# Splitting the input weights of layer 1's mixer ahead of time and reading the parts back from DRAM, in a two-layer diffusion trunk

## The chip, the core and the metric

The kernel runs on one core of a Trainium2 chip. The metric is device time in microseconds (us) of one execution; lower is better. The engines are PE (TensorE), DVE (VectorE), ACT (ScalarE), POOL (GpSimd) and SP (SyncE). SP computes nothing here; it issues most of the DMAs. All DMAs of the core run on 16 DMA engines.

## What is computed

The reference is a trunk of two layers over 512 latent tokens and 256 context tokens of width 1024, all in float32. Cut to what matters here:

```python
def odd_mixer(hl, hc, w_in, ...):                  # layer 1; w_in is 1024 x 2048
    gate_l, xr_l = jnp.split(hl @ w_in, 2, axis=-1)
    gate_c, xr_c = jnp.split(hc @ w_in, 2, axis=-1)
    xr_l, xr_c = depthwise_conv(xr_l, ...), depthwise_conv(xr_c, ...)
    for d, reverse in ((0, False), (1, True)):     # gated linear recurrence over time
        a_c, u_c = rglru_inputs(xr_c, ...); h_c = rglru_scan(a_c, u_c, 0, reverse)
        a_l, u_l = rglru_inputs(xr_l, ...); hs_l.append(rglru_scan(a_l, u_l, h0, reverse))
    y_lat = (gelu(gate_l) * (hs_l[0] + hs_l[1])) @ w_out

def trunk_layer(x, xc, ...):
    y_l, y_c = mixer(modulate(x), modulate(xc))
    x = layer_norm(ALPHA * x + g1 * y_l)
    x = layer_norm(ALPHA * x + g2 * (square(relu(modulate(x) @ mlp_w1)) @ mlp_w2))
    ...                                            # layer 0 does the same for the context xc
```

Layer 0's mixer is attention beside an RWKV-7 scan, layer 1's the recurrent block above. Each layer ends with a squared-ReLU feed-forward of width 4096.

## The kernel before

**Products.** Every large product runs as three: each float32 operand is split into a high part, rounded to PE's fp32r format, and a low part, the rest; `mm3` (L174) adds high by high, low by high and high by low. A weight comes in tiles of 1024 x 128, that is 128 partitions x 8 x 128, 512 KB. `w_raw` (L149) loads a tile into a buffer `wraw` by a DMA of SP, whose pieces are rows of 512 bytes. `w_split` (L155) makes the parts by `split` (L125): ACT casts to `whi`, DVE subtracts into `wlo`. There are 2 buffers `wraw` and 3 each of `whi` and `wlo`. `w_tiles` (L163) does this tile after tile and calls `fill` behind each.

**Layer 1's mixer** (`layer1_mixer`, L549) takes the 16 tiles of `l1_w_in` as they are needed: 8 for the x branch (`xt`, function `dense`, 768 tokens) and 8 for the gate (`gt`, function `gate`, 512 tokens). Block b of 128 channels goes from `dense` (PE), copies into `xp` (ACT), a convolution (`cy`, ACT and DVE), a split of its result, four small products (`tr`, PE), tanh, exp and sqrt (`ga`, `gx`, `tv`, ACT, with table loads between them), and multiplications and scans (DVE). The gate tile of the block is multiplied in at the end, `ge`.

**Fillers.** Work that belongs to a later stage is kept in a list, `self.fillers`; `fill` takes one entry each time that a weight tile has been split. In layer 0's feed-forward the entries are 40 steps of `mods_dve` (L260), which work out a part of layer 1's modulation on DVE (`macc`), from `mraw` tiles. `paced` puts each step behind the last product that was recorded:

```python
def paced(self, gen):
    with self.tc.issue_after(self.pace.ins):
        next(gen)
```

It ties an instruction of the step to that product on the engine of the product, PE; what a step puts on ACT, DVE, POOL or SP isn't tied.

**What sets the order.** The program is recorded in the order of the code, and a scheduler with a timeline of its own then orders each engine's instructions by when it holds them ready. Each engine runs its list strictly in order, and an instruction at the head that waits for a semaphore holds all behind it, DMA issues too.

**The stage around 800 to 930 us.** The RWKV scan of layer 0 ends there. `out_proj` (L697) follows in two halves of 384 tokens, 8 weight tiles of `l0_w_out` each. Behind each half stands `ln_half` (L368), the layer norm: per 128 tokens statistics on DVE, `lnrs` (a power, on POOL), `xn` (ACT), transposes (`tr`, PE), then `hf` (ACT), `hhi` and `t` (DVE) and `hlo` (DVE, and POOL for k in 1, 3, 5). Then the feed-forward `mlp` (L399) begins, with `mr` and `uhi` on ACT, `msq` and `ulo` on DVE. At the end of the scan the stage's inputs come back from DRAM (`t<-o_scr`, `t<-tsp`). The pool `mt`, in which the change puts its buffers, opens with this stage.

Of the kernel before, what the change touches and what calls it, by code (L numbers as in the profile page):

```python
# [10 lines left out]
F32 = mybir.dt.float32  # L11
F32R = mybir.dt.float32r
# [5 lines left out]
D = 1024  # L18
# [9 lines left out]
def run(*gens):  # L28

    gens = list(gens)  # L30
    while gens:
        gens = [g for g in gens if next(g, gens) is not gens]


def weave(tc, dense, lead):

    for ins in lead:
        with tc.issue_after(ins.ins):
            next(dense, None)
    run(dense)  # L40
# [13 lines left out]
class Kern:  # L54
# [108 lines left out]
    def w_tiles(self, ap, group=128, eng=("act", "dve")):  # L163

        K, M = ap.shape
        kt = K // 128
        for c0 in range(0, M, group):
            g = min(group, M - c0)
            raw = self.w_raw(ap[:, c0:c0 + g], kt, g)
            for s in range(0, g, 128):  # L170
                yield (c0 + s) // 128, self.w_split(raw[:, :, s:s + 128], *eng)
                self.fill()

    def mm3(self, out, st, mv, ks, first=True, last=True):  # L174

# [334 lines left out]
XW = XO + NC_  # L510

EARLY = {1: 1, 2: 1, 3: 1, 4: 1, 5: 1, 6: 1}
XS, GS, OS = ("act", "dve"), ("act", "dve"), ("act", "dve")
GE, HS, GW = 2, 4, 1
PREG = 2

# [1 line left out]
class L1(Kern):  # L518
# [30 lines left out]
    def layer1_mixer(self, hhi, hlo, ohi, olo, late):  # L549
        nc = self.nc  # L550
        I = self.I
        with self.tc.tile_pool(name="m1", bufs=1, reuse_waits="tile") as m1:
            self.l1_softplus()
            ea, et, ba, bx = self.lru_e
            spans = ((0, NL, 0), (NL, T, XO))
            w_in = I["l1_w_in"]
            cw = self.cols["l1_conv_w"]
            xps = [m1.tile([128, XP], F32, name=f"xp{i}") for i in range(2)]
            for xp in xps:
# [91 lines left out]
                nc.vector.tensor_tensor(out=hs[b], in0=g["gx", 0][:, :NL], in1=g["gx", 1][:, :NL], op=ALU.add)  # L651

            hs, last, prev = {}, {}, [None, None]
            xt, gt = self.w_tiles(w_in[:, D:2 * D], eng=XS), self.w_tiles(w_in[:, 0:D], eng=GS)

            def gates(n):
                for _ in range(n):
# [22 lines left out]
            with self.tc.issue_after(last[7].ins):  # L680
                run(late)
# [859 lines left out]
class Trunk(L1, MLA, RWKV):  # L1541
    def run(self, out):
        nc, tc, I = self.nc, self.tc, self.I
# [21 lines left out]
        with ExitStack() as s0:  # L1565
# [4 lines left out]
            with ExitStack() as s1:  # L1570
# [3 lines left out]
                with ExitStack() as s2:  # L1574
# [3 lines left out]
                    t = tp.tile([128, 8, T], F32, name="t0")  # L1578
# [42 lines left out]
        with ExitStack() as s0:  # L1621
# [3 lines left out]
            with ExitStack() as s1:  # L1625
# [4 lines left out]
                t = tp.tile([128, 8, T], F32, name="t_0")  # L1630
# [15 lines left out]
                spare = chain(*[self.mods_dve(1, b) for b in range(0, MODV, 2)])  # L1646
                self.fillers += [lambda: self.paced(spare)] * (MODV // 2 * 5)
                self.fillers += [lambda b=b: run(self.mods_spare(1, [b])) for b in range(MODV, 16)]
                lnl = []
                t_spill = self.dram.tile([128, 8, NL], F32, name="t_spill")  # L1650

# [19 lines left out]
            t = tp.tile([128, 8, NL], F32, name="t_1")  # L1671
# [26 lines left out]
```

## Time and profile before

| | us |
|---|---|
| median of 3 runs (lowest, highest) | 2102.24 (2087.21, 2103.8) |
| the profiled execution | 2098.16 |
| its span in the trace | 2096.2 |

| engine | busy us | share of the span |
|---|---|---|
| PE | 1933.4 | 92% |
| DVE | 1264.6 | 60% |
| ACT | 828.6 | 40% |
| POOL | 382.4 | 18% |

The span is the stretch of the trace; 1.96 us of the execution lie outside it. Times below count from the span's start. Of the median, the profiled execution is 4.1 us short. PE's clock was granted at 0.962 of full speed on the mean.

### The profile page before, as it was taken

The page shows a single profiled execution, that of the slowest core. Times are in us where ns is not written, and L with a number is a line of the kernel's source. Part 1 is how long each engine was busy: PE and PEld are TensorE (multiplying, and loading weights), DVE is VectorE, ACT ScalarE, POOL GpSimd, SP SyncE. Part 2 cuts the span into 40 slices and gives each one's busy share as a digit, 9 for nine tenths or more (in the row PEclk, how much of TensorE's full clock was granted, in tenths as well). Part 3 has the DMA queues.
Part 4 walks back from the last instruction along what each step waited for, and adds up shares of the span by engine and source line. Part 5 has one row for each costly group of instructions (what it writes and reads, how often), then busy time and mean ns, then how long its engine had stood idle before and what let it go on. Part 6 is the DMA issues. An engine that isn't in the chain of part 4 may idle for free.

```text
span 2096.2 us, 39749 instructions
## 1 busy us (share of the span) xinstructions
PE 1933.4 (92%) x16130; PEld 1729.7 (83%) x16130; DVE 1264.6 (60%) x2532; ACT 828.6 (40%) x1437; POOL 382.4 (18%) x441
## 2 busy tenths in 40 slices
PE   7889788799999997999999999999989889999997
PEld 4667566577777767899999999998877789999997
DVE  4548777647676678775554333447698575444446
ACT  2344242434554443442131221334789444233242
POOL 0346644534435431100000000001000010000000
PEclk8999889799999998999999999999989989999999
DMA  9455534554423218332232222245521663333334
GB/s 347 122 167 191 144 106 129 153 137 127 125 57 95 61 53 264 102 91 81 81 102 84 67 61 61 61 131 152 151 76 56 203 190 101 92 96 96 98 100 146
DMA packets 429303, 249.20 MB, mean 119 GB/s; under 512 B 79376, under 2 KB 414144, under 8 KB 428992
## 3 DMA queue, kind: packets, MB, share of 16 engines
q1 hardware_dynamic: 428648, 245.55, 40.0%
q8 instruction: 127, 2.08, 0.4%
q0 software_dynamic: 288, 1.05, 0.2%
q14 instruction: 56, 0.46, 0.1%
q10 hardware_dynamic: 184, 0.06, 0.0%
HBM read 209.38 MB, written 36.44 MB: 117 GB/s over the span
## 4 chain that ended last, share of the span: by engine, by line
PE 69%; DVE 10%; DMA 8%; ACT 5%; issue 3%; POOL 2%; SPq 2%; DVEq 0%; ACTq 0%; POOLq 0%
PE mm L183 17%; PE mm L184 17%; PE mm L185 17%; PE tr L183 2%; DVE wlo L136 2%; PE tr L184 1%; ACT whi L130 1%; DMA wraw<-in_l_w_out_dram 1%; PE tr L185 1%; PE mm L883 1%; PE mm L874 1%; PE g L1389 1%; DMA st<-rw_pq 1%; PE g L1366 1%; DMA wraw<-in_l_mlp_w_dram 1%
## 5 line engine op out<-in xcount | busy, mean ns | idle before, releaser
L183 PE MATMUL mm<-hhi,whi 128*128 128x384 f32 (+2 forms) x1504 | 489.1, 326 | 2.7 <-DVE msq L427 2.0
L184 PE MATMUL mm<-hlo,whi 128*128 128x384 f32 (+2 forms) x1504 | 485.8, 323 | 0.2 <-DVE hlo L396 0.2
L185 PE MATMUL mm<-hhi,wlo 128*128 128x384 f32 (+2 forms) x1504 | 485.5, 323 | 0.0
L130 ACT CAST whi<-wraw 128x1024 fp32r<-128x1024 f32 x216 | 226.2, 1049 | 529.7 <-PE mm L184 449.0
L183 PE MATMUL mm<-uhi,whi 128*128 128x384 f32 (+1 forms) x1280 | 399.4, 313 | 4.4 <-DVE t L450 4.2
L185 PE MATMUL mm<-uhi,wlo 128*128 128x384 f32 (+1 forms) x1280 | 397.8, 311 | 3.6 <-DVE wlo L136 3.6
L184 PE MATMUL mm<-ulo,whi 128*128 128x384 f32 (+1 forms) x1280 | 397.2, 311 | 1.0 <-DVE ulo L136 1.0
L136 DVE TENSOR_TENSOR wlo<-wraw,whi 128x1024 fp32r<-128x1024 f32 x216 | 267.6, 1240 | 204.4 <-ACT whi L130 202.7
L183 PEld LDWEIGHTS mm<-hhi,whi 128*128 128x128 f32 x1504 | 285.7, 190 | 15.7 <-issue 2.3
L184 PEld LDWEIGHTS mm<-hlo,whi 128*128 128x128 f32 x1504 | 285.7, 190 | 11.2 <-issue 1.4
L185 PEld LDWEIGHTS mm<-hhi,wlo 128*128 128x128 f32 x1504 | 285.6, 190 | 10.5 <-issue 0.2
L183 PEld LDWEIGHTS mm<-uhi,whi 128*128 128x128 f32 x1280 | 243.8, 191 | 6.0 <-DVE t L450 4.4
L185 PEld LDWEIGHTS mm<-uhi,wlo 128*128 128x128 f32 x1280 | 243.3, 190 | 5.8 <-DVE wlo L136 4.9
L184 PEld LDWEIGHTS mm<-ulo,whi 128*128 128x128 f32 x1280 | 243.4, 190 | 1.8 <-DVE ulo L136 1.5
L450 DVE SCALAR_TENSOR_TENSOR t<-mm,g,t 128x256 f32<-128x256 f32 (+2 forms) x200 | 92.9, 481 | 224.9 <-PE mm L185 222.0
L347 POOL TENSOR_TENSOR lnrs<-lnrs,mhalf 128x1 f32<-128x1 f32 x20 | 10.7, 544 | 1010.1 <-DVE lnrs L346 1010.1
L1411 POOL TENSOR_SCALAR ds<-rv,rw_dd 64x64 f32<-64x64 f32 x176 | 84.6, 481 | 158.8 <-DVE rv L1425 148.9
L427 DVE SCALAR_TENSOR_TENSOR msq<-mm,mr 128x384 f32<-128x384 f32 (+1 forms) x128 | 62.3, 487 | 46.8 <-ACT mr L425 46.6
L425 ACT ACTIVATE mr<-mm 128x384 f32<-128x384 f32 (+1 forms) x128 | 55.6, 434 | 85.4 <-PE mm L185 85.3
L130 ACT CAST uhi<-msq 128x384 fp32r<-128x384 f32 (+1 forms) x128 | 58.6, 458 | 75.6 <-DVE msq L427 75.6
L136 DVE TENSOR_TENSOR ulo<-msq,uhi 128x384 fp32r<-128x384 f32 (+1 forms) x128 | 63.0, 492 | 33.1 <-ACT uhi L130 29.5
L1425 DVE SCALAR_TENSOR_TENSOR rv<-z,rw_dd,ds 64x64 f32<-64x64 f32 x176 | 49.7, 282 | 28.0 <-PE z L1423 23.2
(416 smaller groups left out, 3016.4 us busy)
## 6 DMA issues: line engine op xcount, KB each, us to landing
wraw<-in_l_mlp_w_dram SPq DMA_DIRECT2D x148, 512.0 KB
mraw<-in_l_mod_w_dram SPq DMA_DIRECT2D x48, 512.0 KB
wraw<-in_l_w_in_dram SPq DMA_DIRECT2D x36, 512.0 KB
wraw<-in_l_w_out_dram SPq DMA_DIRECT2D x32, 512.0 KB
mw<-in_l_mod_w_dram SPq DMA_DIRECT2D x16, 512.0 KB
wraw<-in_l_mod_w_dram SPq DMA_DIRECT2D x16, 512.0 KB
rw_bk<-pqbk SPq DMA_DIRECT2D x8, 768.0 KB
rw_pq<-pqbk SPq DMA_DIRECT2D x8, 768.0 KB
```

What stands on the lines that cost most here:

```text
L130: nc.scalar.copy(hi, src)
L136: e.tensor_tensor(out=lo, in0=src, in1=hi.bitcast(F32), op=ALU.subtract)
L183: nc.tensor.matmul(out, sh, mh, start=f, stop=False)
L184: nc.tensor.matmul(out, sh, ml, start=False, stop=False)
L185: ins = nc.tensor.matmul(out, sl, mh, start=False, stop=l)
L425: nc.scalar.activation(r, ps, AF.Relu)
L427: nc.vector.scalar_tensor_tensor(out=sq, in0=ps, scalar=0.0, in1=r, op0=ALU.max, op1=ALU.mult)
L450: nc.vector.scalar_tensor_tensor(out=t[:, m, x:y], in0=ps[:, x - a:y - a], scalar=g[:, m, s:s + 1], in1=t[:, m, x:y], op0=ALU.mult, op1=AL ...
L874: nc.tensor.transpose(ps[:, j * 128:(j + 1) * 128], p[:, (j0 + j) * 128:(j0 + j + 1) * 128], self.ident)
L883: nc.tensor.matmul(po[64 * e:64 * e + 64, :256], va[:, k0 // 128 + j, h * 64:(h + 1) * 64], pts[e][:, j, :], start=(j == 0), stop=(j == n ...
L1411: P.tensor_scalar(out=ds[d][H[e]], in0=rv[H[e], i, e, :], scalar1=dn[H[e]], scalar2=None, op0=ALU.mult)
L1425: V.scalar_tensor_tensor(out=rn[H[e], e, :], in0=zu[d][H[e], 1], scalar=dn[H[e]], in1=ds[d][H[e]], op0=ALU.mult, op1=ALU.add)
```

## The change

The 16 tiles of layer 1's `w_in` are no longer loaded and split in the mixer. A generator `presplit` does it before: per tile a load into `praw`, the same cast on ACT (`phi`) and subtraction on DVE (`plo`), and two DMAs that write the parts to a DRAM tensor `w_pre`, [16, 2, 128, 8, 128], in which each partition's part is one row of 4 KB. All three DMAs of a tile are issued on POOL's queue (`nc.gpsimd`), not on SP's. `praw`, `phi` and `plo` have one buffer each. Its 17 steps are queued as paced fillers behind the 40 of before. In the mixer `w_pre` loads `whi` and `wlo` directly, by two DMAs of SP of 512 KB each.

```diff
@@ class Kern, behind w_tiles @@
+    def presplit(self, ap, n):
+        nc = self.nc
+        self.pre = self.dram.tile([n, 2, 128, 8, 128], F32, name="w_pre")
+        sb = lambda tag, dt: self.mt.tile([128, 8, 128], dt, tag=tag, name=self.nm(tag), bufs=1)
+
+        def load(j):
+            raw = sb("praw", F32)
+            nc.gpsimd.dma_start(raw, ap[:, 128 * j:128 * j + 128].rearrange("(k p) c -> p k c", p=128))
+            return raw
+
+        raw = load(0)
+        yield
+        for j in range(n):
+            hi, lo = sb("phi", F32R), sb("plo", F32R)
+            self.split(hi, lo, raw)
+            if j + 1 < n:
+                raw = load(j + 1)
+            for i, x in enumerate((hi, lo)):
+                nc.gpsimd.dma_start(self.pre[j, i], x.bitcast(F32))
+            yield
+
+    def w_pre(self, js):
+        for i, j in enumerate(js):
+            w = [self.wp.tile([128, 8, 128], F32R, tag=t, name=self.nm(t), bufs=self.wbufs[1]) for t in ("whi", "wlo")]
+            for u, x in enumerate(w):
+                self.nc.sync.dma_start(x.bitcast(F32), self.pre[j, u])
+            yield i, w
@@ layer1_mixer @@
-            w_in = I["l1_w_in"]
...
-            xt, gt = self.w_tiles(w_in[:, D:2 * D], eng=XS), self.w_tiles(w_in[:, 0:D], eng=GS)
+            xt, gt = self.w_pre(range(8, 16)), self.w_pre(range(8))
@@ Trunk.run, layer 0's feed-forward, behind the two lines that queue mods_dve and mods_spare @@
+                ahead = self.presplit(I["l1_w_in"], 16)
+                self.fillers += [lambda: self.paced(ahead)] * 17
```

**POOL, layer 0's output projection and first layer norm.** `ulo` is the last split before it, `lnrs` and `hlo` belong to the layer norm. Before, POOL's list reads:

```order
L136 TENSOR_TENSOR ulo1381_9058<-t_0_9056,uhi1380_9057 128x768 x2
L347 TENSOR_TENSOR lnrs1420_9365<-lnrs1420_9365,mhalf_62 128x1
L347 TENSOR_TENSOR lnrs1426_9386<-lnrs1426_9386,mhalf_62 128x1
L347 TENSOR_TENSOR lnrs1432_9407<-lnrs1432_9407,mhalf_62 128x1
L396 TENSOR_TENSOR hlo1384_9088<-hf1437_9426,hhi1383_9087 128x384
L396 TENSOR_TENSOR hlo1384_9088<-hf1440_9443,hhi1383_9087 128x384
L396 TENSOR_TENSOR hlo1384_9088<-hf1443_9460,hhi1383_9087 128x384
L347 TENSOR_TENSOR lnrs1484_9770<-lnrs1484_9770,mhalf_62 128x1
```

After, it reads like this from the write of the third tile's high part on (lines of the changed code: L182 is the load, L193 the writes, L377 `lnrs`):

```order
L193 DMA w_pre_12719<-phi1874_12986 128x1024
L182 DMA praw1876_12990<-in_l1_w_in_dram 128x8x128
L193 DMA w_pre_12719<-plo1875_12987 128x1024
L193 DMA w_pre_12719<-phi1882_13053 128x1024
L377 TENSOR_TENSOR lnrs1420_9365<-lnrs1420_9365,mhalf_62 128x1
L377 TENSOR_TENSOR lnrs1426_9386<-lnrs1426_9386,mhalf_62 128x1
L182 DMA praw1884_13057<-in_l1_w_in_dram 128x8x128
L193 DMA w_pre_12719<-plo1883_13054 128x1024
L193 DMA w_pre_12719<-phi1890_13120 128x1024
L182 DMA praw1892_13124<-in_l1_w_in_dram 128x8x128
L193 DMA w_pre_12719<-plo1891_13121 128x1024
L377 TENSOR_TENSOR lnrs1432_9407<-lnrs1432_9407,mhalf_62 128x1
```

The 48 DMAs of `presplit` now stand between the `ulo` of the scan's end and the second layer norm's first `lnrs`: eleven ahead of the first layer norm's first `lnrs`, the last seven behind its last `hlo`, and the others between its `lnrs` and `hlo`.

**ACT, the same stage.** `whi` are the splits of the output projection's weights, `xn` and `hf` the layer norm's. Before, ACT's list reads:

```order
L130 CAST whi1460_9556<-wraw1459_9554 128x1024
L357 ACTIVATE xn1422_9370<-tr1417_9351,lnnm1421_9368,lnrs1420_9365 128x1024
L357 ACTIVATE xn1428_9391<-tr1423_9372,lnnm1427_9389,lnrs1426_9386 128x1024
L130 CAST whi1464_9591<-wraw1463_9589 128x1024
L357 ACTIVATE xn1434_9412<-tr1429_9393,lnnm1433_9410,lnrs1432_9407 128x1024
L130 CAST whi1468_9626<-wraw1467_9624 128x1024
L390 ACTIVATE hf1436_9421<-tr1435_9414,a1_0B_9040,a1_0G_9039 128x384
L390 ACTIVATE hf1437_9426<-tr1435_9414,a1_0B_9040,a1_0G_9039 128x384
L390 ACTIVATE hf1439_9438<-tr1438_9431,a1_0B_9040,a1_0G_9039 128x384
L130 CAST whi1472_9663<-wraw1471_9661 128x1024
```

After, with `phi` as the presplit's cast, it reads:

```order
L130 CAST whi1452_9517<-wraw1451_9515 128x1024
L130 CAST phi1882_13053<-praw1876_12990 128x1024
L130 CAST whi1460_9556<-wraw1459_9554 128x1024
L387 ACTIVATE xn1422_9370<-tr1417_9351,lnnm1421_9368,lnrs1420_9365 128x1024
L387 ACTIVATE xn1428_9391<-tr1423_9372,lnnm1427_9389,lnrs1426_9386 128x1024
L130 CAST whi1464_9591<-wraw1463_9589 128x1024
L130 CAST phi1890_13120<-praw1884_13057 128x1024
L130 CAST whi1468_9626<-wraw1467_9624 128x1024
L387 ACTIVATE xn1434_9412<-tr1429_9393,lnnm1433_9410,lnrs1432_9407 128x1024
L130 CAST phi1898_13187<-praw1892_13124 128x1024
L420 ACTIVATE hf1436_9421<-tr1435_9414,a1_0B_9040,a1_0G_9039 128x384
L420 ACTIVATE hf1437_9426<-tr1435_9414,a1_0B_9040,a1_0G_9039 128x384
```

Of the 16 casts `phi`, the first stands behind the third `whi` of the output projection, these three around the first half's layer norm, and the last among the first `mr` and `uhi` of the feed-forward's first chunk; between `xn` and `hf` a `phi` has come in.

**SP, the end of layer 0's feed-forward.** The last `wraw` loads of `mlp_w2` lead over to layer 1. Before, SP's list reads:

```order
L152 DMA wraw2065_14511<-in_l0_mlp_w2_dram 128x8x128
L152 DMA wraw2161_15000<-in_l1_w_in_dram 128x8x128
L152 DMA wraw2166_15059<-in_l1_w_in_dram 128x8x128
L1658 DMA t_spill_9885<-t_0_9056 1024x1x384
L152 DMA wraw2171_15118<-in_l1_w_in_dram 128x8x128
L152 DMA wraw2176_15151<-in_l1_w_in_dram 128x8x128
L247 DMA mraw2111_14738<-in_l1_mod_w_dram 128x8x128
L152 DMA wraw2197_15257<-in_l1_w_in_dram 128x8x128
L247 DMA mraw2115_14755<-in_l1_mod_w_dram 128x8x128
```

After, with L201 as the read of a part, it reads:

```order
L152 DMA wraw2113_14640<-in_l0_mlp_w2_dram 128x8x128
L152 DMA wraw2465_16736<-in_l1_w_out_dram 128x8x128
L152 DMA wraw2469_16768<-in_l1_w_out_dram 128x8x128
L1689 DMA t_spill_9885<-t_0_9056 1024x1x384
L201 DMA whi2209_15129<-w_pre_12719 128x1024
L201 DMA wlo2210_15130<-w_pre_12719 128x1024
L201 DMA whi2213_15186<-w_pre_12719 128x1024
L201 DMA wlo2214_15187<-w_pre_12719 128x1024
L201 DMA whi2217_15243<-w_pre_12719 128x1024
L201 DMA wlo2218_15244<-w_pre_12719 128x1024
L277 DMA mraw2159_14867<-in_l1_mod_w_dram 128x8x128
```

In place of one load of 512 KB a tile there are two, into `whi` and `wlo`; the free `wraw` buffers take the first two tiles of layer 1's output projection. In the mixer the same goes on, two loads per tile among the loads of `gwr` and `mraw`.

## Rows read from the trace of the kernel before

**Rows 1.** The page: engines' busy time, and the chain that ended last by engine.
```profile
PE 1933.4 (92%) x16130; PEld 1729.7 (83%) x16130; DVE 1264.6 (60%) x2532; ACT 828.6 (40%) x1437; POOL 382.4 (18%) x441
...
PE 69%; DVE 10%; DMA 8%; ACT 5%; issue 3%; POOL 2%; SPq 2%; DVEq 0%; ACTq 0%; POOLq 0%
```

**Rows 2.** Busy time by stretch; then PE clock, DMA share, GB/s.
```profile
800.00:845.00 45.00, 40.21 (x221) 38.52 (x220) 38.68 (x95) 11.13 (x11) 1.32 (x3) 0.96 0.79 226
845.00:925.00 80.00, 75.42 (x455) 71.78 (x453) 60.34 (x136) 36.45 (x55) 8.58 (x11) 1.00 0.29 82
1500.00:1640.00 140.00, 125.31 (x710) 108.45 (x709) 124.04 (x165) 124.84 (x153) 0.78 (x1) 0.94 0.26 74
1562.90:1601.91 39.01, 37.45 (x194) 33.40 (x193) 34.16 (x44) 36.05 (x45) 0.00 (x0) 1.00 0.19 54
```

**Rows 3.** The same view, 40 us of layer 1's mixer in two pieces.
```profile
1520.00:1540.00 20.00, 13.84 (x99) 11.60 (x97) 20.00 (x31) 19.52 (x27) 0.00 (x0) 0.85 0.35 93
1540.00:1560.00 20.00, 17.57 (x80) 15.20 (x79) 19.57 (x27) 15.19 (x17) 0.00 (x0) 0.81 0.19 53
```

**Rows 4.** The chain, 1400 to 1720 us: start us, us, what.
```profile
1444.50 1.05 ACT whi L130
1445.58 1.23 DVE wlo L136
...
1601.91 1.05 ACT whi L130
```

**Rows 5.** The page's costliest groups: the weight split.
```profile
L130 ACT CAST whi<-wraw 128x1024 fp32r<-128x1024 f32 x216 | 226.2, 1049 | 529.7 <-PE mm L184 449.0
...
L136 DVE TENSOR_TENSOR wlo<-wraw,whi 128x1024 fp32r<-128x1024 f32 x216 | 267.6, 1240 | 204.4 <-ACT whi L130 202.7
```

**Rows 6.** POOL's only two DMAs: timeline, then landing of gbc and of bbc.
```profile
1623.48 0.78 POOL L1677 DMA_DIRECT2D gbc<-in_l_ln_g_dram  x1 [156.13 <-PE tr L185]
1641.88 0.56 POOL L1678 DMA_DIRECT2D bbc<-in_l_ln_b_dram  x1 [17.63 <-DVE gx L643]
...
DMA to landing us min/median/max: 5.3/5.3/5.3
...
DMA to landing us min/median/max: 4.5/4.5/4.5
```

**Rows 7.** Timeline of POOL around layer 0's output projection.
```profile
798.53 2.07 POOL L136 TENSOR_TENSOR ulo<-t,uhi 128x768 fp32r<-128x768 f32 x1 [2.84 <-ACT uhi L130]
844.28 1.07 POOL L347 TENSOR_TENSOR lnrs<-lnrs,mhalf 128x1 f32<-128x1 f32 x2 [43.68 <-DVE lnrs L346]
```

**Rows 8.** Timeline of ACT in the same stretch and behind it.
```profile
872.63 1.05 ACT L130 CAST whi<-wraw 128x1024 fp32r<-128x1024 f32 x1 [3.05 <-PE mm L184]
...
881.95 1.04 ACT L130 CAST whi<-wraw 128x1024 fp32r<-128x1024 f32 x1 [3.48 <-PE mm L184]
...
925.47 0.49 ACT L425 ACTIVATE mr<-mm 128x384 f32<-128x384 f32 x1
926.65 0.51 ACT L130 CAST uhi<-msq 128x384 fp32r<-128x384 f32 x1 [0.69 <-DVE msq L427]
```

**Rows 9.** Who ACT waited for, 790 to 940 us: us in total, times, longest.
```profile
ACT whi L130 <- PE mm L184: 26.9, 8, 7.4
ACT whi L130 <- DMA wraw<-in_l_w_out_dram: 22.1, 7, 8.5
```

**Rows 10.** The chain again: a weight transfer, and a larger one later.
```profile
816.61 5.46 DMA wraw<-in_l_w_out_dram
...
1642.87 10.69 DMA t<-t_spill
```

**Rows 11.** DMA engines, 790 to 940 us in 40 slices: busy tenths, GB/s.
```profile
DMA  9999995864499540531432444314140000096484
GB/s 343 361 294 361 389 239 146 247 175 136 121 293 283 152 140 4 140 107 33 140 90 79 121 133 140 95 45 140 26 120 2 0 0 4 0 260 180 128 239 139
```

**Rows 12.** The products that the paced steps of before put on DVE.
```profile
L276 DVE SCALAR_TENSOR_TENSOR macc<-mraw,sc,macc x224: 333/344/735, 804.8 to 1143.0; 128x128 f32<-128x128 f32 x112
```

More of the change, by code (lines that the diff above doesn't have):

```diff
@@ L512 @@
 EARLY = {1: 1, 2: 1, 3: 1, 4: 1, 5: 1, 6: 1}
-XS, GS, OS = ("act", "dve"), ("act", "dve"), ("act", "dve")
+OS = ("act", "dve")
 GE, HS, GW = 2, 4, 1
```

## The prediction

> **What bounds the kernel now.** I read the page first: PE is busy 92% of the span and carries 69% of the chain that ended last [rows 1], so only a stage in which PE stands can give time back, and one in which it doesn't can only lose. The view by stretch shows both kinds. From 1500 to 1640 us, in layer 1's mixer, PE is busy 125.31 of 140 us, and ACT (124.84) and DVE (124.04) have hardly a gap either [rows 2]. PE's pauses cost twice there: in the 40 us from 1520 it is idle for 6.16 and 2.43 us, and the granted clock is 0.85 and 0.81 of full speed, between the levels of 1.2 and 2.4 GHz [rows 3]. From 845 to 925 us, in layer 0's output projection and layer norm, PE is busy 75.42 of 80 us, and in the 45 us before 40.21, with the DMA engines at a share of 0.79 [rows 2]. There the chain runs through weight transfers of 5.46 us [rows 10].
>
> **Where the moved work lands.** The change names the feed-forward, but the order does not put it there: from the first `praw` to the last `phi` it stands in the output projection, the layer norm and the first products of the feed-forward. The paced steps of before behave alike: their first product on DVE runs at 804.8 us, in the output projection, though the code queues them later [rows 12]. So I price the 16 tiles in the stretch from 800 to 930 us.
>
> **Gain in the mixer.** A split costs ACT 1.05 us and DVE 1.24 us [rows 5]; 16 of each leave, 16.8 and 19.8 us. What counts is what lies on the chain: of these 32 instructions nine pieces do, six casts and three subtractions, from 1444.50 to 1601.91 us [rows 4], 9.72 us in sum. Against that stands PE: over two blocks, 1562.90 to 1601.91, it is idle for 1.56 us [rows 2], 0.78 a block, so the last three casts (3.15 us) give at most 2.3. I take 9.72 - 0.8 = 8.9 us. The far end is all of PE's idle time from 1500 to 1640 (14.7 us), its clock back at 1.00 (6% of 125.31, 7.5 us) and the first pair of the chain, 2.3: 24.5 us. The near end is nothing, if waits for the reads take the place. A read needs a free `whi`; with three of them and some 19.5 us a block of two tiles it has about one block's time for 1 MB, which I take as hidden: SP's 512 KB land in 5.46 us where the engines are busy [rows 10], and the share here is 0.19 to 0.26 [rows 2].
>
> **Cost of the presplit's own chain.** With one `praw`, one `phi` and one `plo`, tile follows tile: load until landed (L), cast 1.05, subtraction 1.24, next load. A tile takes L + 2.3 us. No row shows a load of 512-byte pieces by POOL. Its two loads of the same size in 4 KB rows landed after 5.3 and 4.5 us [rows 6], the lower end; the upper is the 10.69 us of a 2 MB transfer [rows 10]. To choose, I go by the DMA engines. The stretch 845 to 925 moved 82 GB/s at a share of 0.29 [rows 2], so 512 KB in such pieces cost 1.85 us of all engines; the fastest slice nearby reached 389 GB/s [rows 11], so the two writes cost 2.7 us. That is 4.55 us a tile beside the stretch's own 0.29. At the share of the stretch before it, 0.79, a tile takes 4.55 / 0.50 = 9.1 us; I take L = 6.5 and 8.8 us a tile, since that is nearer to the 5.46 us than to the 10.69.
>
> Place it in time. POOL is free at 800.6 and reaches the first `lnrs` at 844.28, two together 1.07 us [rows 7]. The fifth load stands behind these, so it cannot be issued before 845.4, however early the four tiles before are done. The 16th cast then stands at 845.4 + 6.5 + 11 x 8.8 = 948.7 us. ACT comes to its place in the order, behind an `mr` that ends at 925.96 [rows 8], at 926: ACT is late by 22.7 us, and so are `whi`, `xn`, `hf`, `mr` and `uhi`, which are queued behind the casts, the subtractions' neighbours on DVE, and the later `lnrs` on POOL, for which `xn` waits. PE does not feel all of it: in this stage ACT splits weights as soon as PE frees a buffer (26.9 us of waiting for it [rows 9]), two tiles ahead, and PE frees one every 4.66 us (872.63 to 881.95, two tiles [rows 8]). That is 9.3 us of cover. The term is 22.7 - 9.3 = 13.4 us; with L = 4.5 the 16th cast stands at 924.7 and it is 0, with L = 8.0 it is 31.4, with 10.69 it is 63.8.
>
> **Cost to the transfers before 845 us.** The first half of the projection waits for its weights: 22.1 us of ACT's time in seven waits [rows 9]. The engines' own work there is 0.79 x 45 = 35.6 us; four loads (7.4) and seven writes of 512 KB (1.35 each, 9.4) come to it: 52.4 in 45 us, 7.4 too many. Part of that is hidden by DVE, busy for 38.68 of the 45 us [rows 2]. I take 5, between 0 and 7.4. A rule of the Trainium skill bears on this (DMA: Bandwidth & Descriptors, section "Issuing engines are not separate DMA queues"): DMAs issued from POOL run on the same 16 engines as SP's and interleave with them, so another queue buys no bandwidth. If POOL's queue had its own, this term would be 0 and the term before it near 0, and the sum 2089.3; no row here decides it.
>
> **Clock.** In the mixer 8.6 us of idle PE went with 13.84 x 0.15 + 17.57 x 0.19 = 5.4 us of lost clock [rows 3]. Of some 18 us of new idle time, in smaller pieces, I take 3 us, from 0 to 7. The 16.8 us of ACT and 19.8 of DVE themselves cost nothing more: ACT is busy for 36.45 of 80 us, DVE for 60.34 [rows 2]; if DVE had no gaps, all 19.8 would show.
>
> **Sum.** 2098.16 - 8.9 + 13.4 + 5 + 3 = 2110.7 us for the profiled execution, which is 4.1 us short of the median of before; at the median's level 2115 us, 0.6% above. A difference of 1%, 21 us, is about what a measurement of this kernel can tell.
>
> **Rivals.**
> *Hidden.* L stays at 4.5 us and the transfers find gaps: all three costs are 0, and 8.9 us of gain stay: 2089.3, at the median's level 2093. For it speak POOL's load that landed in 4.5 us while the 2 MB transfer ran beside it [rows 6, 10], and the idle DMA slices around 900 us [rows 11]; against it the slices of 0.9 at the beginning.
> *Hidden, and PE gets its whole idle time:* -24.5 us, 2078. The mixer's PE is too near its own limit for that.
> *The loads are slow (slower than before).* Place: POOL's queue and ACT's, 845 to 930 us. From L = 8.0 on the costs are 31.4 + 7.4 + 7 and the sum 2135.1, 2139 at the median's level; at 10.69 it is 2171. What could do it: POOL makes the descriptors, and its two DMAs of 128 rows kept it busy for 0.78 and 0.56 us [rows 6]; a load here has 1024 pieces, and if the time goes with their number, 4.5 to 6.2 us pass before all are under way. Against it: engines may start before the last piece is described. The Trainium skill (SBUF — State Buffer, section "SBUF: two separate sides") adds another cause: while a DVE copy runs in its fast two-port mode, GpSimd can't write descriptors, and a DMA of 0.62 us took 3.1. No row here shows it.
> *The mixer gives nothing back:* reads on SP hold the `gwr` loads behind them, and the gain of 8.9 is 0: 2119.6, 2124 at the median's level. The low DMA share speaks against it.
>
> **Chances.** Forecast 0.43 (2105 to 2127), hidden 0.22, hidden with all of PE's idle time 0.05, slow loads 0.20, no gain in the mixer 0.10. Faster by over 1% is almost the second hidden case alone, 0.06. Slower by over 1%: slow loads, half of the case without gain, and the forecast's upper end, 0.10: 0.35. Within 1%: 0.59. The range from 2088 to 2148 leaves out the second hidden case, the lower end of the first (0.04) and half of the slow loads.
>
> **What would show it.** In the changed trace: POOL's loads from 801 us on, 6 to 7 us from issue to landing, a tile every 8 to 9 us; `phi` among ACT's waits, for DMA, with 15 to 30 us between 800 and 950; the feed-forward's first chunk later by 10 to 25 us; the DMA share from 845 to 945 near 0.8 rather than 0.29. In the mixer: no casts of weights, blocks of 18.5 to 19 us in place of 19.5, and 5 to 12 us less from the last product of the feed-forward to the first of layer 1's output projection. I am wrong if the last `phi` runs by 930 us, or only after 965, or if SP's reads make PE wait.

## The result, and the profile after

The changed kernel takes 2123.81 us (median of 4 runs, 2121.76 to 2132.09) against 2094.9 us before (4 runs, 2087.21 to 2103.8): ratio 1.0161, 95% interval 1.0134 to 1.0189. It is slower by 1.6%, 9 us above the likeliest time and inside the range; the prediction gave slower by over 1% a chance of 0.35. The profiled execution has a span of 2121.8 us (2096.2 before), so 25.6 us are to be found.

The page of the changed kernel, as [rows 1]. PE's share of the chain has fallen from 69% to 63%, and DMA's has risen from 8% to 12%:

```profile
PE 1949.5 (92%) x16130; PEld 1743.3 (82%) x16130; DVE 1265.0 (60%) x2532; ACT 829.5 (39%) x1437; POOL 419.3 (20%) x489
...
q0 software_dynamic: 7200, 26.22, 3.9%
...
PE 63%; DMA 12%; DVE 10%; ACT 5%; SPq 4%; issue 3%; POOL 3%; DVEq 0%; ACTq 0%; POOLq 0%
```

To say where, I cut every trace at the same five events: A, the end of POOL's last `ulo` before the output projection; N, the first `lnrs` on POOL (half of the projection is done); B, the first `mr` of the feed-forward on ACT; C, layer 0's last residual on DVE; D, the first product of layer 1's output projection. The events of the changed kernel, from the timelines of POOL, ACT, DVE and PE (start, duration; A is 794.78 + 2.07):

```profile
794.78 2.07 POOL L136 TENSOR_TENSOR ulo<-t,uhi 128x768 fp32r<-128x768 f32 x1 [2.84 <-ACT uhi L130]
846.00 1.19 POOL L377 TENSOR_TENSOR lnrs<-lnrs,mhalf 128x1 f32<-128x1 f32 x1
900.26 0.48 ACT L455 ACTIVATE mr<-mm 128x384 f32<-128x384 f32 x1
1470.11 0.74 DVE L480 SCALAR_TENSOR_TENSOR t<-mm,g,t 128x128 f32<-128x128 f32 x2 [3.77 <-PE mm L215]
1661.34 0.28 PE L213 MATMUL mm<-uhi,whi 128*128 128x256 f32 x1
```

Differences of such events, in us, for before, the changed kernel and the experiments told below (one profiled execution each; what lies before A, 788.4 to 802.8 us, and behind D, 452 to 463, differs by more than most of the terms sought and is left out):

| kernel | A to N | N to B | B to C | C to D (mixer) |
|---|---|---|---|---|
| before | 43.7 | 45.4 | 555.0 | 190.4 |
| changed | 49.2 | 54.3 | 569.9 | 191.2 |
| split ahead alone | 48.2 | 55.2 | 572.2 | 188.8 |
| reads alone | 45.5 | 45.1 | 556.0 | 193.4 |
| half the reads | 45.7 | 45.1 | 555.5 | 191.9 |
| held back | 42.3 | 45.1 | 555.7 | 187.8 |
| transfers alone | 55.8 | 51.1 | 555.6 | 188.9 |
| splits alone | 47.7 | 51.3 | 554.2 | 189.0 |
| parts made by POOL | 51.6 | 51.7 | 560.8 | 192.5 |
| held, four tiles as before | 43.5 | 45.1 | 555.8 | 188.9 |
| no weight work in the mixer | 43.4 | 46.0 | 554.2 | 191.4 |
| no writes | 49.7 | 46.3 | 564.5 | 188.9 |
| two products, splits | 43.0 | 45.3 | 555.7 | 183.7 |
| two products, reads, held | 43.4 | 45.3 | 554.2 | 180.4 |

So the changed kernel loses 5.5 + 8.9 + 14.9 = 29.2 us from A to C and gains nothing in the mixer (+0.8). The start is 3.75 us earlier and the end 0.7 us shorter: 29.2 + 0.8 - 3.75 - 0.7 = 25.6, the difference of the spans. The five kernels with splits in the mixer and all products (188.8 to 190.4) show how far two executions of the same mixer lie apart: up to 1.7 us.

Around the layer norm, in the windows of [rows 2] (PE, PEld, DVE, ACT, POOL busy; PE clock, DMA share, GB/s), the DMA share went from 0.29 to 0.87 in the 80 us from 845 and PE's busy time from 75.42 to 65.69:

```profile
800.00:845.00 45.00, 38.35 (x208) 36.22 (x207) 36.71 (x90) 11.80 (x12) 6.04 (x9) 0.96 0.96 288
845.00:925.00 80.00, 65.69 (x358) 61.30 (x356) 53.61 (x95) 37.65 (x48) 27.30 (x38) 0.89 0.87 259
```

What ACT waited for from 790 to 940 us (total, times, longest), as [rows 9], and the 16 casts and their loads by tile (duration in ns min/median/max, first and last start; then the loads' landing):

```profile
ACT phi L130 <- DMA praw<-in_l_w_in_dram: 34.1, 13, 8.2
ACT whi L130 <- DMA wraw<-in_l_w_out_dram: 14.3, 8, 3.3
...
ACT whi L130 <- PE mm L214: 3.6, 1, 3.6
```

```profile
L182 POOL DMA_DIRECT2D praw<-in_l_w_in_dram x16: 912/912/1140, 796.8 to 945.5; - x16
L130 ACT CAST phi<-praw x16: 1044/1050/1056, 805.4 to 951.7; 128x1024 fp32r<-128x1024 f32 x16
...
DMA to landing us min/median/max: 4.9/5.9/8.6
```

Before, ACT's largest wait was for PE (26.9 us), ahead of which it stood with the weights, and the next for weight loads (22.1); now the largest is for the loads of the split ahead. DVE waits as well, for the writes: with one buffer `plo`, ten of the 16 subtractions start only when the write of the tile before has landed (DVE's waits, 795 to 990 us):

```profile
DVE plo L136 <- DMA w_pre<-plo: 14.3, 10, 4.1
```

In the chain that ended last, from 797 to 960 us, these writes carry 38.1% and the loads `praw` 11.2%. The last load is issued at 945.5 us, the 16th cast runs at 951.7, and PE feels it in the feed-forward's first chunk (PE's waits, 900 to 985 us):

```profile
PE tr L360 <- ACT xn L387: 5.8, 1, 5.8
PE mm L213 <- DVE msq L457: 4.3, 1, 4.3
PE tr L414 <- DVE t L424: 1.6, 1, 1.6
PE mm L214 <- POOL hlo L426: 1.1, 1, 1.1
```

### The profile page after: what moved, and what is told of

Same layout as the page of the kernel before. It is cut to its first block, busy times and chain, and to the rows that moved or that the text cites. A ratio compares the mean times of both kernels' runs of the same rounds, so it can differ in the third digit from the quotient of the medians.

```text
span 2121.8 us, 39855 instructions
## 1 busy us (share of the span) xinstructions
PE 1949.5 (92%) x16130; PEld 1743.3 (82%) x16130; DVE 1265.0 (60%) x2532; ACT 829.5 (39%) x1437; POOL 419.3 (20%) x489
## 4 chain that ended last, share of the span: by engine, by line
PE 63%; DMA 12%; DVE 10%; ACT 5%; SPq 4%; issue 3%; POOL 3%; DVEq 0%; ACTq 0%; POOLq 0%
PE mm L213 15%; PE mm L215 15%; PE mm L214 15%; DMA w_pre<-plo 3%; SPq L1032 2%; PE tr L213 2%; DMA wraw<-in_l_mlp_w_dram 2%; PE mm L912 1%; PE tr L214 1%; DVE wlo L136 1%; PE tr L215 1%; DMA wraw<-in_l_w_out_dram 1%; PE mm L903 1%; PE g L1418 1%; PE g L1395 1%
## 5 line engine op out<-in xcount | busy, mean ns | idle before, releaser
L130 ACT CAST whi<-wraw 128x1024 fp32r<-128x1024 f32 x200 | 209.5, 1049 | 505.2 <-PE mm L214 418.6
L136 DVE TENSOR_TENSOR wlo<-wraw,whi 128x1024 fp32r<-128x1024 f32 x200 | 248.9, 1246 | 198.5 <-ACT whi L130 196.8
L214 PEld LDWEIGHTS mm<-hlo,whi 128*128 128x128 f32 x1504 | 288.0, 191 | 12.5 <-POOL hlo L426 1.4
L377 POOL TENSOR_TENSOR lnrs<-lnrs,mhalf 128x1 f32<-128x1 f32 x20 | 12.4, 628 | 918.9 <-DVE lnrs L376 859.5
L1454 DVE SCALAR_TENSOR_TENSOR rv<-z,rw_dd,ds 64x64 f32<-64x64 f32 x176 | 49.7, 282 | 27.6 <-PE z L1452 22.8
```

Of the source, the lines that this page charges most:

```text
L130: nc.scalar.copy(hi, src)
L136: e.tensor_tensor(out=lo, in0=src, in1=hi.bitcast(F32), op=ALU.subtract)
L214: nc.tensor.matmul(out, sh, ml, start=False, stop=False)
L1454: V.scalar_tensor_tensor(out=rn[H[e], e, :], in0=zu[d][H[e], 1], scalar=dn[H[e]], in1=ds[d][H[e]], op0=ALU.mult, op1=ALU.add)
```

## The experiments

Each ratio is taken against the kernel before, run again beside the experiment; its median was 2089.3 to 2094.0 us, so an expected time is read as a distance from it.

**Each half alone.** The first kernel keeps the split ahead, and the mixer goes back to its own splits (nobody reads the parts):

```
-            xt, gt = self.w_pre(range(8, 16)), self.w_pre(range(8))
+            xt, gt = self.w_tiles(w_in[:, D:2 * D]), self.w_tiles(w_in[:, 0:D])
```

Expected: 

> The 16 tiles are split ahead and written to DRAM, but nobody reads them: layer 1's mixer loads and splits its weights as before. Theory (the whole loss is the early stage): 2094.9 + 29.2 = 2124 us, with the stretch from the last ulo on POOL to the last residual of layer 0 at some 673 us (644 before) and the mixer at 190.4. Rival (the mixer does gain its 8.9 us, and the loss before it is hidden in how the segments were cut): 2132 us.

Measured: 2117.18 us, ratio 1.0115 (1.0084 to 1.0146). From A to C 675.6 us, the mixer 188.8. The kernel before took 2092.35 here, so the loss is 24.8 us, where the theory has 29.2 and the rival 37. By the events the loss is the early stage; by the times it is some 4 us shorter than the changed kernel's 28.9, which the intervals can't tell from nothing.

The second keeps the reads and splits only one tile ahead:

```
-                ahead = self.presplit(I["l1_w_in"], 16)
+                ahead = self.presplit(I["l1_w_in"], 1)
-                self.fillers += [lambda: self.paced(ahead)] * 17
+                self.fillers += [lambda: self.paced(ahead)] * 2
...
-                self.nc.sync.dma_start(x.bitcast(F32), self.pre[j, u])
+                self.nc.sync.dma_start(x.bitcast(F32), self.pre[0, u])
```

Expected: 

> Only one tile is split ahead, and the mixer reads this one pair of parts 16 times in place of 16 pairs (so its products use the wrong weights for 15 tiles). Theory (the mixer gives nothing back even without the early chain): 2094 to 2097 us, mixer segment 190 to 192. Rival (the gain of 8.9 us is there, but the shifted feed-forward takes it away again): 2086 us, mixer segment some 182.

Measured: 2091.51 us, ratio 0.9998 (0.9979 to 1.0017); the mixer takes 193.4 us. Reading parts in place of splitting is worth nothing that shows.

**Half the bytes.** The same, with one read a tile:

```
-            w = [self.wp.tile([128, 8, 128], F32R, tag=t, name=self.nm(t), bufs=self.wbufs[1]) for t in ("whi", "wlo")]
-            for u, x in enumerate(w):
-                self.nc.sync.dma_start(x.bitcast(F32), self.pre[0, u])
-            yield i, w
+            w = self.wp.tile([128, 8, 128], F32R, tag="whi", name=self.nm("whi"), bufs=self.wbufs[1])
+            self.nc.sync.dma_start(w.bitcast(F32), self.pre[0, 0])
+            yield i, [w, w]
```

Expected: 

> As the run with reads alone, but only the high part is read and used for the low part too (the third product uses the wrong operand), so that the mixer's reads move as many bytes as before. If the doubled bytes take the gain back (late reads behind the 1 MB pairs): 2084 to 2088 us and a mixer segment of 180 to 183. If PE itself bounds the mixer: no better than reads alone, within 2 us.

Measured: 2092.45 us, ratio 1.0000 (0.9985 to 1.0015); mixer 191.9. The doubled bytes are not what takes the gain back.

**The split ahead held back.** `paced` only ties instructions of PE's own engine, and the split ahead has none, so it drifts to the front. Here its steps are tied to ACT's and DVE's last instructions of the feed-forward in place of PE's:

```
+    def held(self, gen):
+        with self.tc.issue_after(self.paceA.ins), self.tc.issue_after(self.paceV.ins):
+            next(gen)
...
-                    nc.scalar.activation(r, ps, AF.Relu)
+                    self.paceA = nc.scalar.activation(r, ps, AF.Relu)
...
-                self.fillers += [lambda: self.paced(ahead)] * 17
+                self.fillers += [lambda: self.held(ahead)] * 17
```

Expected: 

> The change whole, but every step of the split ahead is also held behind ACT's last relu and DVE's last square of the feed-forward, so that casts and subtractions stand in its second half instead of around the first layer norm. Theory (the place is what costs): the stretch from the last ulo to the last residual falls from 673 to 644 to 650 us, total 2095 to 2101. Rival (the work costs wherever it stands, since each cast waits for its load in ACT's order): 673 again, total 2115 to 2124.

Measured: 2086.56 us (10 runs), ratio 0.9983 (0.9964 to 1.0002); A to C 643.2 us against 644.1 before. The whole loss is gone, with the same instructions and the same bytes; against the kernel before no gain is left that this measurement could show. The casts by tile, and the window in which they lie:

```profile
L130 ACT CAST phi<-praw x16: 1037/1052/1055, 1213.8 to 1343.5; 128x1024 fp32r<-128x1024 f32 x16
```

```profile
1200.00:1431.55 231.55, 231.20 (x1370) 229.44 (x1368) 118.55 (x185) 78.54 (x105) 35.60 (x53) 1.00 0.65 198
```

PE is busy for 231.20 of 231.55 us there, beside a DMA share of 0.65: the feed-forward's second half has room for every load, write, cast and subtraction. A tile still takes (1343.5 - 1213.8) / 15 = 8.6 us, and DVE waits 19.5 us in 14 waits for the write of `plo`, but PE doesn't wait for any of it.

**The stage's loss, taken apart**, always with the mixer's own splits. Transfers alone: no cast, no subtraction, each loaded tile written out twice.

```
-            hi, lo = sb("phi", F32R), sb("plo", F32R)
-            self.split(hi, lo, raw)
+            old = raw
+            for i in range(2):
+                nc.gpsimd.dma_start(self.pre[j, i], old)
...
```

(with two `praw` buffers.) Expected: 

> The 16 loads and 32 writes of the split ahead alone, early as in the change: each loaded tile is written out twice as it is, with no cast and no subtraction (so what lies in DRAM isn't the parts), and the mixer splits its own weights as before. Theory (the loss comes of casts and subtractions that wait for their loads in ACT's and DVE's order): only the transfers' own price is left, 2092.4 + 5 = 2097 us, the stretch to the last residual of layer 0 some 649 us. Rival (the DMA engines' bandwidth is what the stage lacks): 2112 to 2118 us, some 670.

Measured: 2107.56 us, ratio 1.0092 (1.0073 to 1.011). The loss, 17.8 us by the events, lies wholly before B (12.1 before N, 5.7 behind); from B to C it is 0.6. Against its own kernel before, 2089.29, that is 18.3 us more, near the rival's 20 to 26 and far from the theory's 5, but it lies where neither had it: all in the projection and the layer norm, nothing in the feed-forward. The transfers stand closer together here than in the change: with no split between them, 6 loads and 12 writes are issued before N, not 4 and 7.

Splits alone: one load, 16 splits of the same tile, one write.

```
-            if j + 1 < n:
-                raw = load(j + 1)
-            for i, x in enumerate((hi, lo)):
-                nc.gpsimd.dma_start(self.pre[j, i], x.bitcast(F32))
+            if j == n - 1:
+                for i, x in enumerate((hi, lo)):
+                    nc.gpsimd.dma_start(self.pre[j, i], x.bitcast(F32))
```

Expected: 

> The 16 casts and 16 subtractions alone, early as in the change: one tile is loaded, split 16 times, and written once (so the parts of 15 tiles are not made), and the mixer splits its own weights as before. Theory (16.8 us of ACT and 19.8 us of DVE fit into gaps when they wait for no load): 2092 to 2097 us. Rival (DVE has no gaps there): up to 19.8 more, 2112 us.

Measured: 2099.91 us, ratio 1.0044 (1.0025 to 1.0063); 9.9 us before B, -0.8 from B to C. So the 36.6 us of ACT and DVE do not all fit into gaps: an amount like half of DVE's 19.8 us shows, where DVE was busy for 38.68 of 45 us before; that it is DVE's part and not ACT's isn't shown. All 16 casts have started by 868 us here. The losses of the two parts before B (17.8 and 9.9) add up to more than the changed kernel's 14.4, so neither can be read as its share.

No writes: all loads and splits, only the last tile written.

```
-            for i, x in enumerate((hi, lo)):
+            for i, x in enumerate((hi, lo)) if j == n - 1 else ():
```

Expected: 

> The 16 loads, casts and subtractions early as in the change, but only the last tile's parts are written; the mixer splits its own weights as before. With a third of the bytes a load lands sooner: by the sum of the prediction a tile of 4.5 to 5 + 2.3 us puts the 16th cast near 925 to 932 us, and the time lost in the feed-forward falls from 14.9 to 0 to 5 us, the time lost ahead of it from 14.3 to some 10 (that of the splits alone), total 2100 to 2104. Rival (the casts' place in ACT's order costs it whatever the DMA engines do): 14 us in the feed-forward still, 2113 to 2117.

Measured: 2107.73 us, ratio 1.0065 (1.0033 to 1.0097). Loads land after 4.8 us (median), the 16th cast runs at 928.8 us, as the sum had it; the feed-forward still loses 9.5 us, between the two theories. Ahead of it 6.9 are lost, 6.0 of them before N and 0.9 from N to B, where the changed kernel loses 8.9:

```profile
L130 ACT CAST phi<-praw x16: 1038/1048/1056, 806.3 to 928.8; 128x1024 fp32r<-128x1024 f32 x16
```

```profile
PE tr L360 <- ACT xn L387: 4.1, 1, 4.1
PE mm L213 <- DVE msq L457: 2.7, 2, 2.4
```

These are PE's waits from 893 to 980 us, in the same two places as in the changed kernel. The loss in the feed-forward needs casts and subtractions that wait for transfers: the transfers alone (0.6) and the splits alone (-0.8) don't have it. With the writes gone 9.5 of the 14.9 us are left; the rest goes with the writes, for which the subtractions of the changed kernel wait.

**Parts made by POOL**, so that ACT and DVE wait for no load:

```
-            self.split(hi, lo, raw)
+            self.split(hi, lo, raw, "pool", "pool")
```

Expected: 

> The change whole and early, but POOL makes both parts, so that neither ACT nor DVE has an instruction that waits for a load. Theory (their order is what held the stage): 2097 to 2102 us, the stretch to the last residual at some 650. Rival (POOL's own order now holds the layer norm's lnrs, six of them, each behind a load of some 6 us): 2110 us or more.

Measured: 2114.48 us, ratio 1.012 (1.0095 to 1.0146). The rival's time, but not by its mechanism: DVE waits for `lnrs` for only 3.0 us (2.4 before), and from B to C the loss is 5.8, against 14.9. Before B it loses 14.3, as the changed kernel does (14.4); the transfers alone lost 17.8 there. How the loss divides between transfers and DVE isn't shown, but DVE itself took longer beside a computing POOL. The groups by line, 803 to 1000 us (mean ns after the busy time), here and then before:

```profile
L306 DVE SCALAR_TENSOR_TENSOR macc<-mraw,sc,macc 128x128 f32<-128x128 f32 x112 | 42.6, 438 | 0.0
...
L422 DVE CAST hhi<-hf 128x384 fp32r<-128x384 f32 x16 | 10.7, 670 | 4.3 <-ACT hf L420 4.3
...
L276 DVE SCALAR_TENSOR_TENSOR macc<-mraw,sc,macc 128x128 f32<-128x128 f32 x112 | 32.3, 346 | 0.0
...
L392 DVE CAST hhi<-hf 128x384 fp32r<-128x384 f32 x16 | 7.0, 439 | 1.2 <-ACT hf L390 1.0
```

The means hide two groups. Of the 112 `macc` 104 take at most 365 ns, as before; eight take 0.85 to 2.49 us, and each of these overlaps an instruction that POOL computes. So do the five of the 16 `hhi` over 365 ns. One of them starts inside POOL's subtraction and ends 0.2 us behind it:

```profile
877.36 2.40 POOL L136 TENSOR_TENSOR plo<-praw,phi 128x1024 fp32r<-128x1024 f32 x1
877.80 2.19 DVE L422 CAST hhi<-hf 128x384 fp32r<-128x384 f32 x1 [0.89 <-ACT hf L420]
```

**The mixer's start.** In the changed kernel the granted clock falls early in the mixer, to 0.91 and 0.83, where before it was 1.00 for 80 us; the first two windows of 20 us behind C, before and changed:

```profile
1444.67:1464.67 20.00, 17.19 (x166) 14.10 (x165) 12.16 (x37) 9.81 (x20) 3.62 (x5) 1.00 0.53 150
1464.67:1484.67 20.00, 18.22 (x145) 14.78 (x143) 12.52 (x28) 9.88 (x22) 1.24 (x7) 1.00 0.63 174
...
1470.11:1490.11 20.00, 17.18 (x157) 13.93 (x155) 10.23 (x33) 8.03 (x16) 3.56 (x5) 0.91 0.59 192
1490.11:1510.11 20.00, 17.77 (x126) 14.93 (x118) 11.16 (x28) 7.46 (x21) 1.30 (x8) 0.83 0.69 201
```

To bring the start back, the held version with the first two tiles of each half loaded and split as before:

```
...
+            xt = chain(self.w_tiles(w_in[:, D:D + 256]), self.w_pre(range(10, 16), 2))
+            gt = chain(self.w_tiles(w_in[:, 0:256]), self.w_pre(range(2, 8), 2))
...
```

Expected: 

> The held version, but the mixer's first four tiles (two of each half) are loaded and split as before, and only the other twelve are split ahead and read in parts. Theory (the gain is lost where the first reads, 1 MB a tile, land late, hold the loads of mraw behind them on SP's queue, and the granted clock falls to 0.91 and 0.83 in the mixer's first 40 us): the clock there is 1.00 again as before, the mixer segment 182 to 185, total 2080 to 2083 us. Rival (PE and the clock bound it anyway): as the held run, 188 and 2086.

Measured: 2088.18 us, ratio 0.9994 (0.9977 to 1.0012). The clock is 1.00 again for the first 80 us, and the mixer still takes 188.9: the theory has the clock, the rival the time.

**No weight work at all**: one tile is loaded and split, and serves for all 16.

```
...
+            one = next(self.w_tiles(w_in[:, 0:128]))[1]
+            xt, gt = (iter([(b, one) for b in range(8)]) for _ in range(2))
```

Expected: 

> No split ahead, and in layer 1's mixer one weight tile is loaded and split once and used for all 16 (so 15 tiles use wrong weights): what the mixer takes when weights cost ACT, DVE and the DMA engines nothing. Theory (the blocks are at PE's own limit and the start at the scans' and the layer norm's pace, so that splitting was never worth much): mixer segment 185 to 189 us against 188.7 to 190.4 with the split, total 2087 to 2091. Rival (the gain of 8.9 us or more was there, and the late reads took it): 176 to 181, total 2079 to 2083.

Measured: 2088.78 us, ratio 0.9980 (0.9956 to 1.0003), mixer 191.4. With the cost of the weights at zero the mixer is as long as with it, and longer than theory and rival had it. Alone this run doesn't settle the gain: the granted clock is lower at the start than before, which costs 17.89 x 0.09 + 17.88 x 0.17 = 4.6 us by the prediction's way of counting, and the total leaves room for up to 9 us. The run before it has the clock at 1.00 there, twelve of the 16 splits out of the mixer, no shorter mixer and a total that leaves room for less than 5 us. Taken together they show that the 8.9 us were not there. The windows of its first two stretches of 20 us, of two in the middle and of a steady one:

```profile
1439.21:1459.21 20.00, 17.89 (x161) 14.73 (x160) 11.38 (x34) 9.55 (x19) 3.61 (x5) 0.91 0.50 140
1459.21:1479.21 20.00, 17.88 (x133) 14.80 (x133) 11.97 (x30) 8.19 (x22) 1.23 (x7) 0.83 0.55 157
...
1499.21:1519.21 20.00, 19.67 (x137) 17.83 (x136) 14.59 (x24) 19.91 (x26) 0.00 (x0) 1.00 0.16 46
1519.21:1539.21 20.00, 15.73 (x94) 13.41 (x93) 19.38 (x30) 16.47 (x24) 0.00 (x0) 0.93 0.27 79
...
1579.21:1599.21 20.00, 19.46 (x103) 17.61 (x102) 16.85 (x24) 16.22 (x21) 0.00 (x0) 1.00 0.00 1
```

Late reads of weights cannot be what lowered the clock at the start (0.91, 0.83): here there are none. In the steady window PE is busy for 19.46 of 20 us with the DMA engines at rest, and ACT's last two copies of `xp` in a block now wait for PE, as in the changed kernel:

```profile
1580.07 0.54 ACT L605 COPY xp<-mm 128x128 f32<-128x128 f32 x2 [2.08 <-PE mm L215]
...
1599.13 0.54 ACT L605 COPY xp<-mm 128x128 f32<-128x128 f32 x2 [2.08 <-PE mm L215]
```

A block is 19.06 us between these rows, 19.43 before (1583.43 to 1602.86): 0.4 us, for the last three or four blocks. Ahead of them the chain (start, us, what) runs through the recurrence itself, gates on ACT, then scans and convolution on DVE, to the `cyh` that PE waits for, and through no tile of `w_in`:

```profile
1505.19 1.50 ACT tv L653
1506.71 1.83 DVE tv L670 x2
...
1515.43 1.26 DVE gx L672
1516.75 1.06 DVE cy L620 x2
...
1519.15 0.47 DVE cyh L134
1519.76 0.71 PE tr L213 x2
```

**PE relieved.** In two kernels the mixer's 16 tiles are multiplied without the product of the high weights with the activation's low part, once with the splits as before, once held and read in parts:

```
-            nc.tensor.matmul(out, sh, ml, start=False, stop=False)
+            if not two:
+                nc.tensor.matmul(out, sh, ml, start=False, stop=False)
...
```

Expected with splits: 

> As before the change (no split ahead), but the mixer's 16 weight tiles are multiplied with two products in place of three (the one of the weight's high part with the activation's low part is left out), which takes 37 us from PE in the mixer: 64 products of 768 columns at 0.35 us and 64 of 512 at 0.23. Theory (PE stands at the front and hid what the splits cost; with it out of the way ACT, busy for 18.6 of 20 us in a steady stretch, and DVE, 18.4, set the blocks): the mixer falls by only 10 to 20 us, to 170 to 180, blocks of 18 to 18.6 us. Rival (PE alone sets everything): by 30 to 37 us, 153 to 160.

Expected with reads: 

> The held version of the change, with the same product left out of the mixer. Theory (the split's price is there, but PE hides it): the mixer is 8 to 13 us shorter than in the run with two products and splits, blocks of 16.5 to 17 us (ACT 17.2 and DVE 16.9 of 20 before PE is relieved). Rival (scans and their order set the mixer's pace, not the splits): within 3 us of that run.

Measured: 2091.23 us, ratio 0.9995 (0.9971 to 1.002), and 2082.67 us, ratio 0.9965 (0.9941 to 0.9988). The medians differ by 8.6 us. The two kernels set beside each other, ten runs each, differ by 8.3 us on the mean, 3 to 13 with 95%: with PE relieved, reads in place of splits do save time. By the events (one execution each) leaving out the product takes 24.0 us from PE's busy time in the mixer (171.3 to 147.3), not 37, as the granted clock falls there from 0.96 to 0.88; it shortens the mixer by some 6 us, and reads in place of splits by 3.3 more, not 8 to 13. In the last two blocks the price of the splits shows: from one block's last copy `xp` to the next it is 18.1 and 20.6 us with splits, 15.5 and 17.6 with reads (19.6 and 19.4 before). Between the fifth and the sixth block time is lost again: 35.7 us with splits, 38.8 with reads, 25.5 before. With reads, from 80 to 100 us after C, PE works for 7.00 us at the lower of the two clock levels (0.50) and waits for DVE's `cyh` for 9.9 us at once:

```profile
1524.27:1544.27 20.00, 7.00 (x20) 4.86 (x19) 18.47 (x28) 14.85 (x17) 0.00 (x0) 0.50 0.15 45
```

```profile
PE tr L217 <- DVE cyh L134: 9.9, 1, 9.9
```

## Why the prediction was right or wrong

**Placing** was right: the split ahead stands around the layer norm, and holding it back in the feed-forward's second half removes 29 of 29 us. This is the cause of the slowdown, shown by an edit of nothing but the order.

**The presplit's own chain** (forecast 13.4 us, from L = 6.5 and a tile every 8.8 us, 16th cast at 948.7) was right in time: loads land after 5.9 us, the casts follow each other after (951.7 - 853.0) / 11 = 8.97 us from the fifth on, and the 16th stands 105.7 us behind N, against 948.7 - 844.28 = 104.4 in the sum. But its links were not as forecast. By the sum a tile takes L + 2.3 us, here 8.2; the rest is the write of `plo`, for which no term stood: it has to land before the one buffer is free again, and DVE waits 14.3 us for it. And the cover of 9.3 us is the first of the two steps that failed. The term was worked out for all that lies behind N, so that its likeness to the 14.9 us from B to C is luck; from N to C the loss is 8.9 + 14.9 = 23.8 us. The 16th cast is late by 105.7 - (926 - 844.28) = 24.0 us, and nothing of the cover shows. Without the writes the 16th cast comes 81.7 us behind N, no later than ACT's place in the order before, so the sum gives nothing; 10.4 us were lost from N to C. Each earlier cast or subtraction that waits holds `xn`, `mr` and `msq` too.

**The transfers before 845 us** (forecast 5): from A to N the changed kernel loses 5.5 us, with 4 loads and 7 writes issued, as the sum had it. How much of it is the transfers' isn't shown, since the splits alone lose 4.0 there. Alone the transfers cost 12.1, but with 6 loads and 12 writes, so the bound of 7.4 is not tested by it. The extra queue on POOL bought nothing that would cancel the term, which agrees with the rule of the Trainium skill that the prediction weighed (DMA: Bandwidth & Descriptors, section "Issuing engines are not separate DMA queues"): the share went to 0.96 and the loss came.

**The stretch from N to the first relu** had no term of its own beside that chain and 3 us of clock. It lost 8.9. Both halves do it alone, the transfers 5.7 and the splits 5.9, in a stretch whose own DMA share was 0.29 [rows 2]; without the writes it is 0.9. In the changed kernel PE waits for ACT's `xn` for 3.8 and 3.5 us at once from 846 to 900 us, where before it waits for `xn` for 2.3 us in five waits from 846 to 900: what delays ACT or DVE shows there. The clock is in it: granted at 0.89 in the 80 us from 845, 1.00 before, it costs 65.69 x 0.11 = 7.2 us by the prediction's way of counting, the upper end of its 0 to 7. No run separates it from the waits.

**The gain in the mixer** (forecast -8.9, nine pieces of the chain) measured +0.8, and this is the other step that failed. The chain named what came last at nine places; what came next-to-last was 0.4 us behind in the steady blocks (PE, 19.46 of 20 us) and, in the first 100 us, the recurrence, as the chain of the run without weight work shows. Blocks of 18.5 to 19 us, a sign that the prediction named, did come at the end (19.1 and 18.9, from 19.6 and 19.4), and the mixer was no shorter. I had priced PE's own limit for the last three blocks only, and taken the other pieces at full length. The rival without a gain gave 2124 us, the measured time, but its mechanism, reads that hold the loads of `gwr`, is refuted: half the bytes, or none, change nothing. Its time came by luck, too: it stands 21.4 us above the kernel before, where 25.5 were measured between the profiled executions.

Summed: -8.9 + 13.4 + 5 + 3 = 12.5 us forecast, +0.8 + 14.9 + 5.5 + 8.9 = 30.1 measured, less the 4.5 us at both ends that differ between executions. That the time lies inside the range is in part luck: the forecast stood on a median of 2102.24 us before the change, and with the fourth run it is 2094.9. Between medians the change costs 28.9 us, more than twice the 12.5.

**Open:** why the granted clock falls in the mixer's first 40 us. It is 0.91 and 0.83 with reads, with half the reads, with no weights, and also with two products and splits; it is 1.00 before and with four tiles split as before. No kernel here tells what tips it; the held kernels with and without the fall take 187.8 and 188.9 us in the mixer, so it didn't decide its length. A second buffer `plo`, which would take the wait for its write away, was not tried: there is no room for one.

## What to carry to other kernels

Work that is moved "into" a stage goes where its dependences and queues let it; tie it on every engine that executes it, and look at the order, not at the code. A chain names who came last, not how far behind the next one is: before pricing a gain, remove the work altogether once (here one tile for all 16) and see whether the stage gets shorter. Follow a chain through its way out as well: here a single buffer made each tile wait for the write of the one before. Choose the place by the engines that take the work: in the projection's first half DVE was busy for 38.68 of 45 us and the DMA share was 0.79, and the same work cost 29 us from there on that cost nothing in the feed-forward's second half, where DVE is busy for half of the time and PE doesn't wait for the parts.

## What was not expected of the hardware

POOL's issue of a load took 0.912 us against 0.534 to 0.586 for a write of 128 rows, and the loads landed after 4.9 to 8.6 us, where the weight transfer of [rows 10] took 5.46. The prediction took such a load for 1024 pieces, with 4.5 to 6.2 us of issue if the time goes with their number. Nothing like it was seen, but its premise isn't shown either: before, the profile counts 288 packets for POOL's two DMAs of 128 rows, and 7200 with the 48 of the change. That is 144 a DMA, loads and writes alike:

```profile
q0 software_dynamic: 288, 1.05, 0.2%
```

Nor did any of these issues take longer than 1.14 us, so the lock-out of descriptor writing by DVE copies that the prediction took from the Trainium skill (SBUF — State Buffer, section "SBUF: two separate sides") doesn't show here; no row here tells whether such a copy ran beside an issue. DVE instructions became longer while POOL computed on tiles: from 346 to 438 ns for `macc` and 439 to 670 for the cast to `hhi` on the mean, which is not all of them by a little but a few by up to 2.1 us. And 24 us less of PE's busy time in a stage in which PE is busy for 90% of the time gave some 6 us, with a clock of 0.50 in one window: PE's busy time was not its bound.
